# Where matmul inputs begin in SBUF: a pad in the first block, rows of 784 columns in the second, and one wider matmul at its end

## The chip, the cores and the metric

One core of a Trainium2 chip runs the whole kernel. The metric is the device time of one execution in microseconds (us). Three runs of the kernel before gave 3038.32, 3041.43 and 3042.83 us; the median is 3041.43 us.

## What is computed

Two transformer blocks stand one after the other, in float32. The first has two layers over 512 tokens of width 1024; each has a mixer (latent attention, pooling, gating) and a SwiGLU feed-forward of 2816 inner features:

```python
for l in range(DEPTH):
    h = rmsnorm(x, mix_norm[l])
    ...
    x = x + jnp.einsum('bsn,nd->bsd', mix, w_o[l])
    h = rmsnorm(x, ffn_norm[l])
    g = jnp.einsum('bsd,df->bsf', h, w_gate[l])
    u = jnp.einsum('bsd,df->bsf', h, w_up[l])
    x = x + jnp.einsum('bsf,fd->bsd', jax.nn.silu(g) * u, w_down[l])
```

The second has two layers over 256 context tokens and 512 latent tokens together, each input shifted and scaled by a condition vector; the last layer gives latent tokens alone:

```python
x = x + g2 * rmsnorm_2(swiglu(modulate(x, norm_g[l, 2], sh2, sc2), ffn_w_in[l], ffn_w_out[l]), norm_g[l, 3])
if need_ctx:
    ctx = ctx + cg2 * rmsnorm_2(swiglu(modulate(ctx, ...), ffn_w_in[l], ffn_w_out[l]), norm_g[l, 3])
```

## The kernel before, in words

Features lie on the 128 partitions, tokens along the row. Every float32 operand is held as a high and a low part (`h` and `l`, type float32r), and each product is three matmuls: high weight by high input, high by low, low by high (`mm`, L329 to L331, in the first block; `mm2`, L993, in the second; `sums`, L1542, and `first2`, L961, for parts of the tokens at a time). The stationary operand is a 128x128 block of weights, the moving operand 256, 258 or 512 tokens. Weights stream in through `wload`: a DMA into `raw`, ScalarE writes `whi`, VectorE `wlo`, two buffers of each. TensorE's order is written out by hand; the order on the other engines comes from a scheduler.

Where things begin in a row of SBUF (bytes within a partition, as the built program places them):

- **Weights.** The pool starts at 19968 = 39x512 and its tiles are 4096 bytes, so every block of 128 weights begins at a multiple of 512.
- **First block.** Mixer inputs `hah`/`hal` start at 48640 = 95x512, 2048 bytes each: multiples of 512. The feed-forward inputs `hbh`/`hbl` and inner features `hidh`/`hidl` stand in a pool that is stacked from the right under `blk1` (x, bt, acc: 20480 bytes under 229344), so all of them begin 480 bytes past a multiple of 512. The mixer's query tiles `qh`/`ql` begin 160 past one.
- **Second block.** `hh` and `hl` hold 8 rows (one for each 128 features) of 770 columns: 256 context tokens, 2 columns for the shift vectors, 512 latent tokens. A row is 3080 bytes = 6x512+8, so row k of `hh` begins 8k past a multiple of 512 and row k of `hl` 64+8k; latent tokens begin at column 258, 8 bytes further. `mm2` runs over `SEG`: 258 columns (context and shifts), then 512 (latent); over `SEGL`, in latent-only stages: 258 (shifts and 256 tokens), then 256.
- **Inner features of the second block** are arena tiles `t` of 780 columns; context and latent parts are written with the same two-column gap, so the parts begin at 64j and at 64j+8 past a multiple of 512.

In `ffn2` the down projection of the latent-only layer runs over `hseg` of two times 256 columns, into two PSUM banks (`mmtile`), although both halves have the same weights.

Of the kernel before, what the change touches and what calls it, by code (L numbers as in the profile page):

```python
# [9 lines left out]
F32 = mybir.dt.float32  # L10
# [7 lines left out]
P = 128  # L18
S = 512
SC = 256  # L20
T2 = S + SC
KD = 8
NF = 22
EPS = 1e-6
# [231 lines left out]
class Body:  # L256
# [171 lines left out]
    def mixer1(self, l, h, acc):  # L428
# [6 lines left out]
        W = S + 16  # L435
        X = lambda n=S, dt=F32: p.tile([P, W], dt, tag="t", bufs=XS, name=self.nm("t"))[:, :n]
        vcol = lambda n, j: self.vec1[:, vb + V1[n] + j:vb + V1[n] + j + 1]
        rc = T("rc", 1, (P, 8))

        def column(dst, src):  # L440

# [114 lines left out]
        def attend(h_, qp, po):  # L556


            j, hh = h_ // 2, h_ % 2
            (qh, ql), kt = qT[h_], kT[h_]  # L560
            prs = []
            for q in range(2):
                pss = self.aux()
                s = slice((2 * qp + q) * P, (2 * qp + q + 1) * P)
                self.mm(pss, qh[:, s], ql[:, s], kt[0], kt[1], True, True)
                sc = T("smx", 6, (P, 4))
                nc.vector.tensor_reduce(sc[:, 0:1], pss, AX.X, ALU.max, negate=True)
                pr = X()
                nc.scalar.activation(pr, pss, AF.Exp, bias=sc[:, 0:1], accum_out=sc[:, 1:2])
                nc.vector.reciprocal(sc[:, 2:3], sc[:, 1:2])  # L570
                if q == 0:
                    nc.scalar.activation(pr, pr, AF.Copy, scale=sc[:, 2:3])
                else:
                    nc.gpsimd.tensor_tensor(pr, pr, sc[:, 2:3].to_broadcast([P, S]), ALU.mult)
                prs.append(pr)
            yield
            yield
            pth, ptl = R("pth", 3, (P, 4, 256)), R("ptl", 3, (P, 4, 256))
            for q, pr in enumerate(prs):
                pt = self.aux()  # L580
                for k in range(4):
                    nc.tensor.transpose(pt[:, k * P:(k + 1) * P], pr[:, k * P:(k + 1) * P], self.ident)
                s = slice(q * P, (q + 1) * P)
                self.split(pth[:, :, s], ptl[:, :, s], pt.rearrange("p (k q) -> p k q", k=4))
            yield
            if qp == 0:
                po[h_] = self.aux()
            s = slice(qp * 256, qp * 256 + 256)
            for k in range(4):
                for e, pt in enumerate((pth, ptl)):  # L590
                    nc.tensor.matmul(po[h_][:, s], vv[:, k, h_ * P:(h_ + 1) * P], pt[:, k, :],
                                     start=(k == 0 and e == 0 and qp == 0), stop=(k == 3 and e == 1), skip_group_check=True)
            if qp == 1:
                t, pv = X(), po.pop(h_)
                o, o2 = slice(64 * hh, 64 * hh + 64), slice(64 - 64 * hh, 128 - 64 * hh)
                nc.scalar.activation(t[o], pv[o2], AF.Copy)
                nc.vector.tensor_tensor(t[o], pv[o], t[o], ALU.add)
                self.split(h[j][0][o], h[j][1][o], t[o], nc.gpsimd)
# [199 lines left out]
    def run(self):  # L798
# [4 lines left out]
        self.x = [xall[:, k, :] for k in range(KD)]  # L803
        self.bt = pb.tile([P, S], F32, tag="bt", name="bt")
        acc = pb.tile([P, S], F32, tag="acc", name="acc")
        ea = ExitStack()
        pa = ea.enter_context(tc.tile_pool(name="ha", bufs=1))
        ha = [(pa.tile([P, S], F32R, tag=f"hah{k}", name=f"hah{k}"), pa.tile([P, S], F32R, tag=f"hal{k}", name=f"hal{k}"))
# [83 lines left out]

    def shift2(self, l, m):
        sh = self.ada[l][:, m * 8:m * 8 + 8, :]
        self.split(self.hh[:, :, SC:SC + 2], self.hl[:, :, SC:SC + 2], sh)

    def squares2(self, k, x, o, w, acc, tmp=None):

# [12 lines left out]
    def feed2(self, k, x, o, w, l, n):  # L911

        for c, s in ((0, 1), (SC, 0)):
            a, b = max(o, c), min(o + w, (SC, T2)[1 - s])
            if a < b:
                h = a + (0, 2)[1 - s]
                self.split_scaled(self.hh[:, k, h:h + b - a], self.hl[:, k, h:h + b - a], x[:, a - o:b - o],
                                  self.mod[l][n][:, k, s:s + 1])

# [10 lines left out]
            nc.scalar.activation(acc[:, a:a + 256], ps[:, :256], AF.Ln, scale=1.0 / div, bias=self.epsc)  # L930
        nc.scalar.activation(acc[:, o:o + w], acc[:, o:o + w], AF.Exp, scale=-0.5)  # L931

    SEG = ((0, SC + 2), (SC + 2, S))
    SEGL = ((SC, SC + 2), (2 * SC + 2, SC))

    def proj2(self, seg, key, u=0):

# [4 lines left out]
        self.mm2(ps, wh, wl, 0, [(self.hh[:, k, :], self.hl[:, k, :]) for k in range(KD)], seg)  # L942
        return ps

    PART = ((0, 0, 0, SC + 2), (1, 0, SC + 2, SC), (1, SC, 2 * SC + 2, SC))
    PARTL = ((0, 0, SC, SC + 2), (1, 0, 2 * SC + 2, SC))

    def first2(self, parts, units, pend):

# [36 lines left out]
    def mm2(self, ps, wh, wl, off, xs, seg):  # L986
        t = self.nc.tensor
        n = len(xs)
        for k, (xh, xl) in enumerate(xs):
            s = slice(off + k * P, off + (k + 1) * P)  # L990
            for w, x, st, en in ((wh, xh, k == 0, False), (wh, xl, False, False), (wl, xh, False, k == n - 1)):
                for b, (o, w_) in enumerate(seg):
                    t.matmul(ps[:, b, :w_], w[:, s], x[:, o:o + w_], start=st, stop=en, skip_group_check=True)  # L993
            self.tick()
# [38 lines left out]
    def mixer_ab(self, r):  # L1033
# [420 lines left out]
        def place(h):  # L1454

            for a, n in ((0, 2), (2, 4)):
                hc = (slice(0, SC), slice(SC + 2, T2 + 2))[a // 2]
                self.split(self.hh[:, h, hc], self.hl[:, h, hc], gates[h][0][:, a * P:(a + n) * P])

        for h in range(3):  # L1460
# [16 lines left out]
        for h in range(8):  # L1477
# [1 line left out]
                for _ in finish(h):  # L1479
                    pass  # L1480
            place(h)
        return [(self.hh[:, h, :], self.hl[:, h, :]) for h in range(8)]

    SEGM = ((0, SC), (SC + 2, S))

    def post(self, ys, off, o, w, acc, mod, feed, sums=None):

# [41 lines left out]
    def sums(self, ws, xs, o, w):  # L1529

        t = self.nc.tensor
        ps = [self.aux() for _ in ws]
        n = len(xs)
        for ks in (range(n - 1), range(n - 1, n)):
            for p, (wh, wl, off) in zip(ps, ws):
                for k in ks:
                    xh, xl = xs[k]
                    s = slice(off + k * P, off + (k + 1) * P)
                    for i, (a, x) in enumerate(((wh, xh), (wh, xl), (wl, xh))):
                        for b in range(0, w, SC):  # L1540
                            c = o + b + (0, 2)[o + b >= SC]
                            t.matmul(p[:, b:b + SC], a[:, s], x[:, c:c + SC], start=(k == 0 and i == 0 and b == 0),  # L1542
                                     stop=(k == n - 1 and i == 2), skip_group_check=True)
                    self.tick()
        return [p[:, :w] for p in ps]
# [18 lines left out]
    def ffn2(self, l, r, seg, lat, parts, acc, post):  # L1564
# [3 lines left out]
        if lat:  # L1568
            cols = ((slice(SC, 2 * SC), 0, 2, 0), (slice(2 * SC, T2), 1, 0, 0))
            bcol = slice(0, 2)  # L1570
            hseg = ((SC + 2, SC), (2 * SC + 2, SC))
        else:
            cols = ((slice(0, SC), 0, 0, 1), (slice(SC, T2), 1, 0, 0))
            bcol = slice(SC, SC + 2)
            hseg = self.SEGM
        hid = []

        def unit(f):
# [13 lines left out]
            for c, b, p0, s in cols:  # L1592
                n = c.stop - c.start
                nc.vector.tensor_tensor(u[:, c], pu[:, b, p0:p0 + n], r[:, c], ALU.mult)
                nc.vector.scalar_tensor_tensor(a[:, c], u[:, c], bu[:, s:s + 1], a[:, c], ALU.add, ALU.mult)  # L1595
                h0 = hseg[b][0]
                self.split(hi[:, h0:h0 + n], lo[:, h0:h0 + n], a[:, c])
            hid.append((hi, lo))

        f = 0  # L1600
        for gi, g in enumerate(GROUPS):
# [6 lines left out]
            for d in range(0, KD, 2):  # L1608
                wh, wl = self.wload("w2", ("d", l, gi), d // 2, 2 * g * P)
                for i in range(2):  # L1610
                    ps = self.mmtile()
                    self.mm2(ps, wh, wl, i * g * P, hid[:g], hseg)
                    k = d + i
                    if gi == 0:
                        ys[k] = self.T()
                    for c, b, p0, s in cols:
                        n = c.stop - c.start
                        if gi == 0:
                            nc.scalar.activation(ys[k][:, c], ps[:, b, :n], AF.Copy)
                        else:  # L1620
                            nc.vector.tensor_tensor(ys[k][:, c], ys[k][:, c], ps[:, b, :n], ALU.add)
# [22 lines left out]
    def mixer_c(self, r):  # L1644
# [96 lines left out]
        held = []  # L1741

        def store(h, o):
            hc = slice(SC + 2, T2 + 2)
            self.split(self.hh[:, h, hc], self.hl[:, h, hc], o)

        def attend(h, qp):
# [54 lines left out]
        for n in range(2 * 16 + 4):  # L1802
# [7 lines left out]
                store(*held.pop(0))  # L1810
            if n == 1 or n % 4 == 0 and 0 < n <= 20:
                late.pop(0)()
        return [(self.hh[:, h, :], self.hl[:, h, :]) for h in range(8)]

    def arena(self, name, slots, width=780):
        es = ExitStack()
        self.ar = es.enter_context(self.tc.tile_pool(name=name, bufs=1, reuse_waits="tile"))
        self.nslots = slots
# [3 lines left out]
    def second_begin(self):  # L1822
# [2 lines left out]
        self.e2 = ExitStack()  # L1825
        pb = self.e2.enter_context(tc.tile_pool(name="blk2", bufs=1, reuse_waits="tile"))
        self.dr = self.e2.enter_context(tc.tile_pool(name="dram", bufs=1, space=bass.MemoryType.DRAM))
        self.hh = pb.tile([P, KD, T2 + 2], F32R, tag="hh", name="hh")
        self.hl = pb.tile([P, KD, T2 + 2], F32R, tag="hl", name="hl")
        self.accs = [pb.tile([P, T2], F32, tag=f"acc{i}", name=f"acc2{i}") for i in range(2)]  # L1830
        es = ExitStack()
        p = es.enter_context(tc.tile_pool(name="ctx0", bufs=1, reuse_waits="tile"))
# [9 lines left out]
    def second(self, xall, pf, hb, acc, ef, eb):  # L1842
# [57 lines left out]
        self.drain()  # L1900
        ea.close()

        ea = self.arena("ffn20", 25)
        self.ffn2(0, n0, self.SEG, False, ((0, SC), (SC, SC), (S, SC)), na,
                  lambda ys, o, w: self.post(ys, 0, o, w, na, self.mod[0][3], feed(1, 0), n0))
        self.first2(self.PART, (("ck", 0), ("ck", 1)), norms)
# [17 lines left out]
        self.drain()  # L1924
        ea.close()

        ea = self.arena("ffn21", 26)

        def store(k, x, o, w):
            if k % 2:  # L1930
# [36 lines left out]
```

## Time and profile before

| | us |
|---|---|
| median of three runs | 3041.43 |
| profiled execution, its own time | 3047.24 |
| its span in the trace | 3045.4 |
| TensorE (PE) busy in the span | 2920.7 |
| VectorE (DVE) busy | 1862.0 |
| ScalarE (ACT) busy | 1191.7 |

The profiled execution is 5.8 us above the median, and 1.8 us of it lie outside the span. Matmuls overlap in the trace: the next one starts before the shown end of the one ahead, so how fast they follow each other is read from starts, over a stretch with a known number of them.

### The profile page before, as it was taken

What the parts mean: (1) busy time and instruction counts of PE and PEld (TensorE: products, weight loads), DVE (VectorE), ACT (ScalarE), POOL (GpSimd) and SP (SyncE); (2) the same over time, 40 slices, a digit from 0 to 9 for tenths busy, and PEclk for the clock granted to TensorE, in tenths of its full rate; (3) what the DMA queues carried; (4) which work ended last, traced back from release to release, by engine and by line L of the source; (5) the groups of instructions that cost most, each with busy time, mean ns of one, the idle gap of its engine ahead of it and who ended that gap; (6) DMA issues with size and microseconds to landing.
All of it is one profiled execution on the core that took longest, in us unless ns stands there. A gap on an engine that the chain in (4) does not pass through costs nothing. (4 is left out here: it accounts for less than half of the span.)

```text
span 3045.4 us, 42771 instructions
## 1 busy us (share of the span) xinstructions
PE 2920.7 (96%) x17002; PEld 2499.6 (82%) x17002; DVE 1862.0 (61%) x3253; ACT 1191.7 (39%) x2088; POOL 550.1 (18%) x434
## 2 busy tenths in 40 slices
PE   9989999999999999899999989999999899999997
PEld 7777888777778888766767888888889788899997
DVE  7679974476689965746554653333344778544445
ACT  5663222346642223432325543221123577532222
POOL 3630000046310001432233140000001420300002
PEclk9999999999999999899999999999999999999999
DMA  4236653232156632210121302212221210223322
GB/s 150 63 103 191 208 159 97 87 107 63 56 190 209 206 124 97 72 42 28 35 66 60 106 20 70 63 63 63 63 63 63 81 43 13 91 94 93 95 91 70
DMA packets 85112, 278.49 MB, mean 91 GB/s; under 512 B 9968, under 2 KB 15344, under 8 KB 84400
## 3 DMA queue, kind: packets, MB, share of 16 engines
q1 hardware_dynamic: 84912, 275.76, 28.6%
q8 instruction: 134, 2.20, 0.3%
q14 instruction: 66, 0.54, 0.1%
HBM read 264.84 MB, written 6.68 MB: 89 GB/s over the span
## 5 line engine op out<-in xcount | busy, mean ns | idle before, releaser
L302 ACT ACTIVATE whi<-raw 128x1024 fp32r<-128x1024 f32 (+1 forms) x363 | 377.7, 1041 | 1289.7 <-PE b L993 472.3
L993 PE MATMUL b<-hh,whi 128*128 128x258 f32 x2000 | 491.1, 327 | 0.0
L993 PE MATMUL b<-hl,whi 128*128 128x258 f32 x2000 | 470.9, 317 | 0.0
L993 PE MATMUL b<-hh,wlo 128*128 128x258 f32 x2000 | 469.7, 316 | 0.0
L303 DVE TENSOR_TENSOR wlo<-raw,whi 128x1024 fp32r<-128x1024 f32 (+1 forms) x321 | 398.0, 1240 | 108.9 <-ACT whi L302 107.5
L993 PEld LDWEIGHTS b<-hh,whi 128*128 128x128 f32 x2000 | 339.8, 190 | 45.3 <-issue 23.8
L993 PEld LDWEIGHTS b<-hl,whi 128*128 128x128 f32 x2000 | 351.3, 190 | 26.1
L993 PEld LDWEIGHTS b<-hh,wlo 128*128 128x128 f32 x2000 | 350.7, 189 | 26.7
L330 PE MATMUL b<-hbl,whi 128*128 128x512 f32 x704 | 279.3, 397 | 3.5 <-DVE hbl L341 3.5
L329 PE MATMUL b<-hbh,whi 128*128 128x512 f32 x704 | 279.8, 398 | 0.8 <-ACT hbh L340 0.8
L331 PE MATMUL b<-hbh,wlo 128*128 128x512 f32 x704 | 279.3, 397 | 0.7 <-DVE wlo L303 0.7
L859 DVE SCALAR_TENSOR_TENSOR junk<-araw,cond 128x1024 f32<-128x1024 f32 x192 | 238.6, 1243 | 4.7 <-DMA araw<-ada 1.9
L1527 POOL TENSOR_TENSOR acc<-acc,t 128x256 f32<-128x256 f32 (+1 forms) x54 | 48.9, 906 | 1018.3 <-ACT t L1522 1017.4
L993 PE MATMUL b<-t,whi 128*128 128x256 f32 (+1 forms) x1152 | 217.3, 311 | 0.0
L993 PEld LDWEIGHTS b<-t,whi 128*128 128x128 f32 x1152 | 178.1, 190 | 12.6
L388 POOL TENSOR_TENSOR acc<-acc,sq 128x512 f32<-128x512 f32 (+1 forms) x33 | 44.4, 1346 | 786.3 <-ACT sq L385 785.8
L330 PEld LDWEIGHTS b<-hbl,whi 128*128 128x128 f32 x704 | 132.5, 188 | 36.7 <-DVE hbl L341 4.2
L329 PEld LDWEIGHTS b<-hbh,whi 128*128 128x128 f32 x704 | 132.7, 188 | 33.6 <-ACT hbh L340 1.2
L331 PEld LDWEIGHTS b<-hbh,wlo 128*128 128x128 f32 x704 | 132.6, 188 | 33.5 <-DVE wlo L303 1.6
L303 POOL TENSOR_TENSOR wlo<-raw,whi 128x1024 fp32r<-128x1024 f32 x42 | 105.3, 2510 | 249.1 <-ACT whi L302 194.7
L331 PE MATMUL b<-hidh,wlo 128*128 128x512 f32 (+1 forms) x352 | 136.0, 386 | 1.6 <-DVE wlo L303 1.6
L329 PE MATMUL b<-hidh,whi 128*128 128x512 f32 (+1 forms) x352 | 135.7, 386 | 0.0
(444 smaller groups left out, 5805.1 us busy)
## 6 DMA issues: line engine op xcount, KB each, us to landing
raw<-w SPq DMA_DIRECT2D x365, 512.0 KB, 3.6
araw<-ada SPq DMA_DIRECT2D x96, 512.0 KB, 4.1
raw<-w SPq DMA_DIRECT2D x18, 256.0 KB, 2.7
xr<-xd SPq DMA_DIRECT2D x2, 2048.0 KB, 8.3
t<-dm SPq DMA_DIRECT2D x8, 384.0 KB, 5.3
x<-xT SPq DMA_DIRECT2D x8, 256.0 KB, 5.2
kTh<-krh SPq DMA_DIRECT2D x32, 64.0 KB, 2.0
kTl<-krl SPq DMA_DIRECT2D x32, 64.0 KB, 2.0
```

The costliest lines, as they stand in the source:

```text
L302: self.last = nc.scalar.activation(hi[:, :m], r, AF.Copy).ins
L303: self.lo_eng.tensor_tensor(lo[:, :m], r, hi[:, :m].bitcast(F32), ALU.subtract)
L329: t.matmul(out, ah, bh, start=start, stop=False, skip_group_check=True)
L330: t.matmul(out, ah, bl, start=False, stop=False, skip_group_check=True)
L331: t.matmul(out, al, bh, start=False, stop=stop, skip_group_check=True)
L388: nc.gpsimd.tensor_tensor(acc[:, c], acc[:, c], t[:, c], ALU.add)
L859: nc.vector.scalar_tensor_tensor(junk, raw, 1.0, self.cond[:, s], ALU.mult, ALU.mult, accum_out=self.ada[l][:, t, s:s + 1])
L993: t.matmul(ps[:, b, :w_], w[:, s], x[:, o:o + w_], start=st, stop=en, skip_group_check=True)
L1527: nc.gpsimd.tensor_tensor(ac, ac, t, ALU.add)
```

## The change

It moves starting addresses, and makes one pair of matmuls a single one. No computed value changes.

1. `run`: a tile of 120 floats (480 bytes) that nothing uses is put below `acc`, so the pool under it begins at 126464 = 247x512. `hbh`, `hbl`, `hidh`, `hidl` now begin at multiples of 512. In `mixer1` two small tiles (`rc`, `smx`) get wider; the query tiles go from 160 to 192 past one.
2. `hh` and `hl` have rows of 784 columns = 3136 bytes = 6x512+64. Context begins at column 14 (`CO`), shifts stand at 270 (`SH`), latent tokens at 272 (`LT`). In row k of either, the 258-column part begins 64k+56 past a multiple of 512, the latent part 64k+64.
3. In the two feed-forwards of the second block the arena tiles are 768 columns without a gap: both parts begin at multiples of 512. Elsewhere the arena's 780 becomes 784.
4. In the latent-only layer `hseg` is one segment of 512 columns and one bank; the evacuation that follows is one instruction over 512 columns.

```diff
+CO, SH, LT, HW = 14, 270, 272, 784
...
+        pb.tile([P, 120], F32, tag="pad", name="pad")
...
-    SEG = ((0, SC + 2), (SC + 2, S))
-    SEGL = ((SC, SC + 2), (2 * SC + 2, SC))
+    SEG = ((CO, SC + 2), (LT, S))
+    SEGL = ((SH, SC + 2), (LT + SC, SC))
...
-    SEGM = ((0, SC), (SC + 2, S))
+    SEGM = ((0, SC), (SC, S))
...
         if lat:
             cols = ((slice(SC, 2 * SC), 0, 2, 0), (slice(2 * SC, T2), 1, 0, 0))
             bcol = slice(0, 2)
-            hseg = ((SC + 2, SC), (2 * SC + 2, SC))
+            hseg, outs = ((SC, S),), ((slice(SC, T2), 0),)
         else:
...
-            hseg = self.SEGM
+            hseg, outs = self.SEGM, ((slice(0, SC), 0), (slice(SC, T2), 1))
...
-                h0 = hseg[b][0]
-                self.split(hi[:, h0:h0 + n], lo[:, h0:h0 + n], a[:, c])
-            hid.append((hi, lo))
+                self.split(hi[:, c], lo[:, c], a[:, c])
+            hid.append((hi, lo, 0, 0))
...
-                    ps = self.mmtile()
+                    ps = self.mmtile() if len(hseg) > 1 else Banks(self.aux())
...
-                    for c, b, p0, s in cols:
+                    for c, b in outs:
...
-    def arena(self, name, slots, width=780):
+    def arena(self, name, slots, width=784):
...
-        self.hh = pb.tile([P, KD, T2 + 2], F32R, tag="hh", name="hh")
-        self.hl = pb.tile([P, KD, T2 + 2], F32R, tag="hl", name="hl")
+        self.hh = pb.tile([P, KD, HW], F32R, tag="hh", name="hh")
+        self.hl = pb.tile([P, KD, HW], F32R, tag="hl", name="hl")
...
-        ea = self.arena("ffn20", 25)
+        ea = self.arena("ffn20", 25, T2)
...
-        ea = self.arena("ffn21", 26)
+        ea = self.arena("ffn21", 26, T2)
```

The order of instructions differs in one place alone, the down projections of the last feed-forward (`ffn2` with `lat`). On TensorE there, before, first output of the second group of inner features (`b` is a PSUM bank, `t` an inner feature's high or low tile):

```order
L993 MATMUL b_23791<-t_23087,whi_23786 128x256
L993 MATMUL b_23792<-t_23087,whi_23786 128x256
L993 MATMUL b_23791<-t_23088,whi_23786 128x256
L993 MATMUL b_23792<-t_23088,whi_23786 128x256
L993 MATMUL b_23791<-t_23087,wlo_23787 128x256
L993 MATMUL b_23792<-t_23087,wlo_23787 128x256
```

The same place on TensorE with the change:

```order
L997 MATMUL b_23728<-t_23088,whi_23723 128x512
L997 MATMUL b_23728<-t_23089,whi_23723 128x512
L997 MATMUL b_23728<-t_23088,wlo_23724 128x512
L997 MATMUL b_23728<-t_23316,whi_23723 128x512
L997 MATMUL b_23728<-t_23317,whi_23723 128x512
```

Each pair of 256 columns into two banks has become one matmul of 512 columns into one bank. On VectorE behind them, before (`t` is now the output being summed):

```order
L1621 TENSOR_TENSOR t_23117<-t_23117,b_23791 128x256
L1621 TENSOR_TENSOR t_23117<-t_23117,b_23792 128x256
L1621 TENSOR_TENSOR t_23134<-t_23134,b_23819 128x256
L1621 TENSOR_TENSOR t_23134<-t_23134,b_23820 128x256
L303 TENSOR_TENSOR wlo_23911<-raw_23909,whi_23910 128x1024
```

And on VectorE with the change:

```order
L1624 TENSOR_TENSOR t_23111<-t_23111,b_23728 128x512
L1624 TENSOR_TENSOR t_23120<-t_23120,b_23742 128x512
L305 TENSOR_TENSOR wlo_23792<-raw_23790,whi_23791 128x1024
L1624 TENSOR_TENSOR t_23135<-t_23135,b_23762 128x512
L1624 TENSOR_TENSOR t_23144<-t_23144,b_23776 128x512
```

Two additions of 256 columns have become one of 512; the weight preparation (`wlo`) stands between the same outputs as before. In all there are 432 matmuls and 32 VectorE additions fewer.

## Rows read from the trace of the kernel before

**Rows 1.** The page's first part: busy time, share of the span, instructions.

```profile
PE 2920.7 (96%) x17002; PEld 2499.6 (82%) x17002; DVE 1862.0 (61%) x3253; ACT 1191.7 (39%) x2088; POOL 550.1 (18%) x434
```

**Rows 2.** Stretches: length; busy PE, PEld, DVE, ACT, POOL; PE clock, DMA share, GB/s.

```profile
245.00:600.00 355.00, 351.21 (x1495) 281.85 (x1496) 251.17 (x357) 95.81 (x113) 1.06 (x1) 1.00 0.47 149
810.00:1215.00 405.00, 403.56 (x1823) 328.46 (x1823) 311.50 (x450) 130.46 (x175) 26.68 (x25) 1.00 0.51 162
1262.00:1720.00 458.00, 438.09 (x2494) 322.23 (x2495) 251.29 (x591) 182.97 (x341) 140.53 (x76) 0.97 0.15 45
1825.00:2360.00 535.00, 534.88 (x3118) 472.26 (x3117) 213.25 (x378) 133.15 (x200) 10.23 (x13) 1.00 0.21 64
2660.00:3005.00 345.00, 345.00 (x2875) 345.00 (x2874) 162.64 (x340) 106.44 (x168) 0.00 (x0) 1.00 0.30 92
```

**Rows 3.** PE's largest wait from 830 to 1190 us: total, times, longest.

```profile
PE b L331 <- DVE wlo L303: 0.9, 2, 0.5
```

**Rows 4.** Stretches of TensorE in the first block that hold 512-column matmuls alone.

```profile
58.84:63.05 4.21, 4.21 (x19) 1.00 0.58 154
63.05:84.59 21.54, 21.54 (x97) 1.00 0.37 115
292.42:605.55 313.13, 313.13 (x1344) 1.00 0.45 143
888.71:1190.17 301.46, 301.46 (x1293) 1.00 0.54 171
```

**Rows 5.** Timeline of TensorE where the first two of these stretches meet.

```profile
62.82 0.39 PE L331 MATMUL b<-qh,wlo 128*128 128x512 f32 x1
63.05 0.39 PE L329 MATMUL b<-hah,whi 128*128 128x512 f32 x1
```

**Rows 6.** Matmul groups by form: tiles, shapes, count, busy us, mean ns.

```profile
L329 PE MATMUL b<-hbh,whi 128*128 128x512 f32 x704 | 279.8, 398 | 0.8 <-ACT hbh L340 0.8
L329 PE MATMUL b<-hidh,whi 128*128 128x512 f32 x320 | 126.6, 395 | 0.0
L993 PE MATMUL b<-hh,whi 128*128 128x258 f32 x1000 | 302.9, 303 | 0.0
L993 PE MATMUL b<-hh,whi 128*128 128x512 f32 x600 | 237.9, 397 | 0.0
L993 PE MATMUL b<-hh,whi 128*128 128x256 f32 x400 | 112.7, 282 | 0.0
L993 PE MATMUL b<-t,whi 128*128 128x256 f32 x864 | 173.9, 283 | 0.0
L993 PE MATMUL b<-t,whi 128*128 128x512 f32 x288 | 107.4, 394 | 0.0
```

**Rows 7.** Stretches of TensorE in the second block's feed-forwards, each of pairs alone.

```profile
1879.39:1946.84 67.45, 67.45 (x385) 1.00 0.21 67
1946.84:1980.60 33.76, 33.76 (x194) 1.00 0.19 63
2691.59:2737.62 46.03, 46.03 (x386) 1.00 0.32 104
2737.62:2760.81 23.19, 23.19 (x194) 1.00 0.30 91
```

**Rows 8.** Feature row 7's pairs, 258+512: sum of 32 stretches, 1886.77 to 2250.41.

```profile
sum 33.28, PE 33.28; mean PE 1.04
```

**Rows 9.** The same for feature row 0, 32 stretches, 1879.39 to 2243.05.

```profile
sum 34.09, PE 34.09; mean PE 1.07
```

**Rows 10.** Feature row 7's pairs, 258+256: sum of 32 stretches, 2696.64 to 2945.12.

```profile
sum 22.86, PE 22.86; mean PE 0.71
```

**Rows 11.** The same for feature row 2, 32 stretches, 2693.03 to 2941.53.

```profile
sum 23.51, PE 23.51; mean PE 0.73
```

**Rows 12.** VectorE's additions to the outputs, 2660 to 3005, and 1860 to 2355 us.

```profile
L1621 DVE TENSOR_TENSOR t<-t,b 128x256 f32<-128x256 f32 x64 | 24.1, 418 | 40.8 <-PE b L993 40.8
L1621 DVE TENSOR_TENSOR t<-t,b 128x512 f32<-128x512 f32 x32 | 21.8, 680 | 0.0
```

More of the change, by code (lines that the diff above doesn't have):

```diff
@@ L437, in mixer1 @@
         vcol = lambda n, j: self.vec1[:, vb + V1[n] + j:vb + V1[n] + j + 1]
-        rc = T("rc", 1, (P, 8))
+        rc = T("rc", 1, (P, 16))
         def column(dst, src):
@@ L565, in attend @@
                 self.mm(pss, qh[:, s], ql[:, s], kt[0], kt[1], True, True)
-                sc = T("smx", 6, (P, 4))
+                sc = T("smx", 6, (P, 16))
                 nc.vector.tensor_reduce(sc[:, 0:1], pss, AX.X, ALU.max, negate=True)
@@ L894, in shift2 @@
         sh = self.ada[l][:, m * 8:m * 8 + 8, :]
-        self.split(self.hh[:, :, SC:SC + 2], self.hl[:, :, SC:SC + 2], sh)
+        self.split(self.hh[:, :, SH:LT], self.hl[:, :, SH:LT], sh)
     def squares2(self, k, x, o, w, acc, tmp=None):
@@ L915, in feed2 @@
             if a < b:
-                h = a + (0, 2)[1 - s]
+                h = a + (LT - SC, CO)[s]
                 self.split_scaled(self.hh[:, k, h:h + b - a], self.hl[:, k, h:h + b - a], x[:, a - o:b - o],
@@ L943, in proj2 @@
         return ps
-    PART = ((0, 0, 0, SC + 2), (1, 0, SC + 2, SC), (1, SC, 2 * SC + 2, SC))
-    PARTL = ((0, 0, SC, SC + 2), (1, 0, 2 * SC + 2, SC))
+    PART = ((0, 0, CO, SC + 2), (1, 0, LT, SC), (1, SC, LT + SC, SC))
+    PARTL = ((0, 0, SH, SC + 2), (1, 0, LT + SC, SC))
     def first2(self, parts, units, pend):
@@ L988, in mm2 @@
         n = len(xs)
-        for k, (xh, xl) in enumerate(xs):
+        for k, (xh, xl, *_) in enumerate(xs):
             s = slice(off + k * P, off + (k + 1) * P)
@@ L1456, in place @@
             for a, n in ((0, 2), (2, 4)):
-                hc = (slice(0, SC), slice(SC + 2, T2 + 2))[a // 2]
+                hc = (slice(CO, SH), slice(LT, HW))[a // 2]
                 self.split(self.hh[:, h, hc], self.hl[:, h, hc], gates[h][0][:, a * P:(a + n) * P])
@@ L1481, in mixer_ab @@
             place(h)
-        return [(self.hh[:, h, :], self.hl[:, h, :]) for h in range(8)]
-    SEGM = ((0, SC), (SC + 2, S))
+        return [(self.hh[:, h, :], self.hl[:, h, :], CO, LT - SC) for h in range(8)]
+    SEGM = ((0, SC), (SC, S))
     def post(self, ys, off, o, w, acc, mod, feed, sums=None):
@@ L1536, in sums @@
                 for k in ks:
-                    xh, xl = xs[k]
+                    xh, xl, *at = xs[k]
                     s = slice(off + k * P, off + (k + 1) * P)
@@ L1540, in sums @@
                         for b in range(0, w, SC):
-                            c = o + b + (0, 2)[o + b >= SC]
+                            c = o + b + at[o + b >= SC]
                             t.matmul(p[:, b:b + SC], a[:, s], x[:, c:c + SC], start=(k == 0 and i == 0 and b == 0),
@@ L1743, in store @@
         def store(h, o):
-            hc = slice(SC + 2, T2 + 2)
+            hc = slice(LT, HW)
             self.split(self.hh[:, h, hc], self.hl[:, h, hc], o)
@@ L1812, in mixer_c @@
                 late.pop(0)()
-        return [(self.hh[:, h, :], self.hl[:, h, :]) for h in range(8)]
-    def arena(self, name, slots, width=780):
+        return [(self.hh[:, h, :], self.hl[:, h, :], CO, LT - SC) for h in range(8)]
+    def arena(self, name, slots, width=784):
         es = ExitStack()
```

## The prediction

> **What bounds the kernel.** I began with busy time: TensorE is busy for 96% of the span [rows 1]. Split by stage, the four feed-forward stretches are the plainest: TensorE is busy for 351.2 of 355, 403.6 of 405, 534.9 of 535 and 345 of 345 us at full clock, while VectorE, the next, has 251.2, 311.5, 213.3 and 162.6 [rows 2]. In the second of them TensorE's largest kind of wait sums to 0.9 us [rows 3]. There the end is set by how fast one matmul follows another; whatever is shortened between starts comes off the time.
>
> So I read the pace, from stretches that hold one kind of matmul and no wait. The number in brackets counts instructions seen in a stretch, one or two more than the intervals. 18 matmuls of 512 columns with inputs `qh`/`ql`, 160 bytes past a multiple of 512, take 4.21 us: 233.9 ns each. The next 96, inputs `hah`/`hal` at multiples of 512, take 21.54 us for 95 intervals: 226.7 ns [rows 4]. They follow each other directly [rows 5]: same weights' buffers, same shape, same clock, other starts. In the feed-forward, inputs at 480 past, 1342 intervals take 313.13 us and 1292 take 301.46: 233.3 ns both times [rows 4]. The weights begin at multiples of 512 in all of them. The reader is to see two paces, 227 and 233 to 234, that go with the starting address.
>
> In the second block the eight feature rows begin at eight offsets, and the pace goes with the row. A pair of 258 and 512 columns takes 67.45 us / 192 = 351.3 ns on the mean [rows 7]; in row 7, whose parts begin at 56 and 64 (`hh`) or 120 and 128 (`hl`), 33.28 / 96 = 346.7 [rows 8]; in row 0, at 0 and 8 or 64 and 72, 34.09 / 96 = 355.1 [rows 9]. Pairs of 258 and 256 take 46.03 / 192 = 239.7 on the mean [rows 7], 22.86 / 96 = 238.1 in row 7 [rows 10], 23.51 / 96 = 244.9 in row 2 [rows 11].
>
> **The change part by part.**
>
> *The pad.* `hb` and `hid` go from 480 to 0 past a multiple of 512, which is where `ha` is. There are 3 x 704 and 3 x 320 = 3072 such matmuls of 512 columns, the named groups standing for a third each [rows 6]. 3072 x (233.3 - 226.7) = 20.3 us. Bounds: nothing, if it is the tiles and not the offset, and this; I take 19.5, since the 226.7 is the best of the `ha` stretches and others may lie some tenths above. VectorE would be busy for 311.5 of some 397 us instead of 405, so nothing else becomes the bound.
>
> *Rows of 784 columns.* Every row now has the 258 part at 56 and the latent part at 0 past a multiple of 64, as only row 7 had before. 3 x 600 = 1800 pairs of 258 and 512 [rows 6] at row 7's pace would give 1800 x 4.6 = 8.3 us; 3 x 400 = 1200 pairs of 258 and 256 would give 1200 x 1.6 = 1.9 us. But row 7 shows only offsets 64 and 128 past a multiple of 512; the new rows also stand at 192 to 448, which no row of before shows for 512 columns. The bounds are row 7's pace for all, and the worst row's: 1800 x (351.3 - 355.1) = -6.8 and 1200 x (239.7 - 244.9) = -6.2 us. Nearest to row 7, but not all of it: 2.8 ns and 1.0 ns a pair, 5.0 and 1.2 us. Of the 1800, 744 are in the mixer (31 projections of 24), where TensorE is busy for 438.1 of 458 us [rows 2] and waits between; I take 1.0 us off for that.
>
> *Inner features without a gap.* In the context layer 432 pairs (288 with `whi` [rows 6], half as many with `wlo`) of 256 and 512 columns take 33.76 / 96 = 351.7 ns [rows 7]. Now both parts begin at multiples of 512: the 512 at 226.7, the 256 at half of a pair of 256 columns, 23.19 / 96 / 2 = 120.8 [rows 7], together 347.5. Gain 4.2 x 432 = 1.8 us, between 0 and that; I take 1.4.
>
> *One matmul for two.* 864 and 432 matmuls of 256 columns, less the 288 and 144 of the context layer [rows 6], are 864 in 432 pairs of 241.6 ns; each becomes one matmul of 512 at 226.7. Gain 14.9 x 432 = 6.4 us; at 233.3 it would be 3.6. I take 6.2.
>
> *Costed at nothing.* 64 VectorE additions of 418 ns become 32 of 680 [rows 12]: 26.8 us against 21.8, under a VectorE that is idle for half of that stretch. A bank is then read 0.68 us after its last matmul instead of 0.42; with eight banks and one filled in 12 x 227 ns = 2.7 us, TensorE doesn't come to wait for it. The pad and the wider small tiles issue nothing. No other instruction moves on any engine.
>
> Sum: 19.5 + 5.0 + 1.2 - 1.0 + 1.4 + 6.2 = 32.3 us. The profiled execution's 3047.2 (span 3045.4 and 1.8 outside it) becomes 3014.9; it lies 5.8 us above the median, so the median 3041.4 becomes 3009.1.
>
> **A rule against it.** Where the 18 and the 96 matmuls meet, the pace changes from 233.9 to 226.7 ns with the address [rows 4, 5]. The Trainium skill (TensorE: Matmul & The Clock Gate, "Step-by-step: what each phase is for") says that TensorE has two independent read ports, so that loading the next weights takes no read bandwidth from the running matmul; by that, where inputs and weights begin relative to each other would not matter. The row disagrees, and decides here; by the rule alone the sum would be the merged matmuls' 3.6 to 6.4 us, the second rival below.
>
> **Rivals.**
>
> *The new rows are bad ones.* For it: paces differ by 8 ns between rows for no reason that the profile names [rows 8, 9], and 192 to 448 are untried. Against: the one class that resembles them is the fastest. If they cost what the worst rows do, 5.0 + 1.2 - 1.0 turns into -13.0: the gain is 14.1 us, 3027.3. Chance 0.10.
>
> *Addresses set nothing; only the matmul count does.* Then `ha` would be faster for what it is, not for where. Against: `qh` beside it [rows 4], and eight paces in eight rows of one tile. Gain 6.2 us, 3035.2. Chance 0.05.
>
> *Equal starts collide, and it gets slower.* Inputs and weights begin alike modulo 512 after the change; far more matmuls would read the same offset at once. Against: `ha` is in that position already, at 226.7. For the whole to be slower by 6.1 us, with the rows' and gaps' terms as above (6.6), 512-column matmuls at offset 0 must cost more than X with 3072 x (X - 233.3) + 432 x (X - 241.6) = 12.7 us, X = 237.9 ns. At 240, 20.6 - 0.7 - 6.6 = 13.3 us more: 3054.7. Chance 0.03.
>
> The forecast has 0.82, and by itself 3002 to 3016: its upper side is rows that give nothing (3014.3) with two us of scatter between runs, its lower side row 7's pace everywhere (3041.4 - 20.3 - 8.3 - 1.9 - 1.8 - 6.4 = 3002.7). The range for 8 in 10 goes from 3001 up to 3019, to hold part of the first rival; what lies above it is the rest of that one and the other two, and some misses below. A measurement of this kernel can tell 0.2%, 6.1 us. Faster by more: the forecast, the first rival and about half of the second, whose 6.2 us stand on the edge: 0.94. Within: 0.03. Slower: 0.03.
>
> **What would show it.** In the feed-forwards of the first block, 512-column matmuls that follow each other every 227 ns; each of those two stretches about 9 to 10 us shorter. In the context layer, 24 pairs of one projection in about 8.36 us instead of 8.43. In the last layer, 96 matmuls of 512 columns in 21.8 us where 96 pairs took 23.2. The order of instructions and the waits stay as they are. The forecast is wrong if `hb` stays at 233 with its new address, or if single rows of `hh` take 355 ns a pair or more; the profile after shows the pace of each row apart.

## The result and the profile after

The kernel after takes 3013.79 us (median of four runs, 3008.93 to 3015.0); the kernel before, run beside it, 3041.23 (3038.32 to 3042.83). The ratio is 0.9906, 95% interval 0.9894 to 0.9918: faster by 0.9%. The profiled execution took 3015.0 us with a span of 3012.8, where that of before had 3045.4: 32.6 us less. The medians differ by only 27.4, because the profiled execution of before lay 6.0 us above the median of these four runs and that of after 1.2 above its own.

The page's first part, busy time of each engine in the kernel after:

```profile
PE 2885.2 (96%) x16570; PEld 2465.0 (82%) x16570; DVE 1861.2 (62%) x3221; ACT 1191.3 (40%) x2080; POOL 548.8 (18%) x434
```

Against [rows 1] TensorE has 432 matmuls fewer and is busy for 35.5 us less; its share is 96% as before. Weight loads (PEld) shrink with it, and VectorE, ScalarE and GpSimd moved by no more than 1.3 us.

Stretches of TensorE alone in the kernel after: length, busy time with the number of instructions seen, granted clock, DMA share, GB/s. The first three answer to [rows 4], the others to [rows 7], in the same order.

```profile
62.23:83.78 21.55, 21.55 (x96) 1.00 0.36 113
288.65:592.86 304.21, 304.21 (x1344) 1.00 0.47 147
875.63:1168.51 292.88, 292.88 (x1294) 1.00 0.54 176
1858.92:1926.22 67.30, 67.30 (x385) 1.00 0.22 68
1926.22:1959.51 33.29, 33.29 (x194) 1.00 0.21 64
2665.56:2711.32 45.76, 45.76 (x386) 1.00 0.33 104
2711.32:2733.10 21.78, 21.78 (x98) 1.00 0.32 96
```

Divide by the intervals, as before. The 95 of `ha` are unchanged at 226.8 ns. In the first block's feed-forwards 304.21 us / 1342 and 292.88 / 1292 give 226.7 ns twice, where 233.3 stood: the two paces have become one. In the second block 67.30 / 192 = 350.5 ns a pair of 258 and 512 columns (351.3 before), 33.29 / 96 = 346.8 a pair of inner features (351.7), 45.76 / 192 = 238.3 a pair of 258 and 256 (239.7), and 21.78 / 96 = 226.9 for one matmul of 512 where 241.6 was paid for two of 256. The 351.7 of before is one of five stretches, and they differ; here are the other four:

```profile
1862.54:1879.39 16.85, 16.85 (x98) 1.00 0.38 108
2048.05:2081.65 33.60, 33.60 (x193) 1.00 0.20 63
2149.12:2182.95 33.83, 33.83 (x194) 1.00 0.20 63
2250.41:2283.92 33.51, 33.51 (x193) 1.00 0.20 63
```

With 48 pairs in the first and 96 in each of the others, they run from 349.1 to 352.4 ns; the mean of all 432 pairs is 350.8.

TensorE's largest wait from 815 to 1168 us in the kernel after (total, times, longest), and the timeline where `qh`/`ql` and `ha` meet:

```profile
PE b L333 <- DVE wlo L305: 2.2, 4, 0.7
```

```profile
61.99 0.39 PE L333 MATMUL b<-qh,wlo 128*128 128x512 f32 x1
62.23 0.39 PE L331 MATMUL b<-hah,whi 128*128 128x512 f32 x1
62.45 0.40 PE L332 MATMUL b<-hal,whi 128*128 128x512 f32 x1
```

The largest kind of wait was 0.9 us in all in [rows 3]: a faster TensorE now waits 1.3 us more for `wlo`, in a stretch of 353 us. Nothing new bounds it. The step from one pace to the other is still there, as in [rows 5].

Matmuls of the inner features as `mm2` issues them, from 1820 us on, and VectorE's additions to the outputs, both in the kernel after:

```profile
L997 PE MATMUL b<-t,whi 128*128 128x512 f32 x576 | 195.1, 390 | 0.0
```

```profile
L1624 DVE TENSOR_TENSOR t<-t,b 128x512 f32<-128x512 f32 x32 | 21.9, 686 | 38.0 <-PE b L997 38.0
```

With `whi` there are 288 + 288 of 512 columns ([rows 6] had 288, and 576 halves more), and the additions of the last layer are 32 of 686 ns, as [rows 12] led one to expect.

### The profile page after: what moved, and what is told of

Same layout as the page of the kernel before. It is cut to its first block, busy times and chain, and to the rows that moved or that the text cites. A ratio compares the mean times of both kernels' runs of the same rounds, so it can differ in the third digit from the quotient of the medians.

```text
span 3012.8 us, 41854 instructions
## 1 busy us (share of the span) xinstructions
PE 2885.2 (96%) x16570; PEld 2465.0 (82%) x16570; DVE 1861.2 (62%) x3221; ACT 1191.3 (40%) x2080; POOL 548.8 (18%) x434
## 5 line engine op out<-in xcount | busy, mean ns | idle before, releaser
L305 DVE TENSOR_TENSOR wlo<-raw,whi 128x1024 fp32r<-128x1024 f32 (+1 forms) x321 | 398.2, 1241 | 103.7 <-ACT whi L304 103.1
L332 PE MATMUL b<-hbl,whi 128*128 128x512 f32 x704 | 275.1, 391 | 3.6 <-DVE hbl L343 3.6
L331 PE MATMUL b<-hbh,whi 128*128 128x512 f32 x704 | 275.6, 391 | 1.0 <-ACT hbh L342 1.0
L333 PE MATMUL b<-hbh,wlo 128*128 128x512 f32 x704 | 274.9, 391 | 0.9 <-DVE wlo L305 0.9
L863 DVE SCALAR_TENSOR_TENSOR junk<-araw,cond 128x1024 f32<-128x1024 f32 x192 | 238.3, 1241 | 7.3 <-DMA araw<-ada 3.7
L997 PEld LDWEIGHTS b<-t,whi 128*128 128x128 f32 x864 | 151.8, 188 | 22.8
L332 PEld LDWEIGHTS b<-hbl,whi 128*128 128x128 f32 x704 | 132.7, 188 | 32.4 <-DVE hbl L343 4.4
L333 PEld LDWEIGHTS b<-hbh,wlo 128*128 128x128 f32 x704 | 132.7, 189 | 29.4 <-DVE wlo L305 1.8
L331 PEld LDWEIGHTS b<-hbh,whi 128*128 128x128 f32 x704 | 132.7, 188 | 29.1 <-ACT hbh L342 1.4
L333 PE MATMUL b<-hidh,wlo 128*128 128x512 f32 (+1 forms) x352 | 134.2, 381 | 2.9 <-DVE wlo L305 2.9
L331 PE MATMUL b<-hidh,whi 128*128 128x512 f32 (+1 forms) x352 | 133.8, 380 | 0.0
```

The source lines that it names most:

```text
L305: self.lo_eng.tensor_tensor(lo[:, :m], r, hi[:, :m].bitcast(F32), ALU.subtract)
L331: t.matmul(out, ah, bh, start=start, stop=False, skip_group_check=True)
L332: t.matmul(out, ah, bl, start=False, stop=False, skip_group_check=True)
L333: t.matmul(out, al, bh, start=False, stop=stop, skip_group_check=True)
L863: nc.vector.scalar_tensor_tensor(junk, raw, 1.0, self.cond[:, s], ALU.mult, ALU.mult, accum_out=self.ada[l][:, t, s:s + 1])
```

## Experiments

What was open: whether the address sets the pace at all, or the tile; whether it is the input's place, or its distance from the weights' place; which modulus counts; and why the rows of 784 columns gave so little. "Place" is the start of the input's row less the start of the weights, in bytes. Paces by place are mean differences between a matmul's start and the next one's in the trace, over intervals without a wait. Dots in an edit stand for lines left out.

**Without the pad**, the rest of the change as it is.

```diff
-        pb.tile([P, 120], F32, tag="pad", name="pad")
```

> The change without its 120-float pad, so hb and hid begin 480 bytes past a multiple of 512 again; all else as in the change. If the address sets their pace: 512-column matmuls of the first block's feed-forwards start every 233.3 ns again and the time rises by 3072 x 6.6 ns = 20.3 us, to about 3034. If it was something else in the change (the wider small tiles, other placements), they stay at 226.7 ns and 3014 us.

Measured 3031.06 us (3028.65 to 3036.43), 0.997 of before (0.9961 to 0.998). The stretches of the first block in this kernel:

```profile
62.42:84.21 21.79, 21.79 (x98) 1.00 0.40 116
291.29:604.66 313.37, 313.37 (x1344) 1.00 0.45 143
887.46:1189.15 301.69, 301.69 (x1294) 1.00 0.53 171
```

One interval more in each than above: 313.37 / 1343 and 301.69 / 1293 = 233.3 ns again, `ha` stays at 227. The pad alone is worth 17.3 us by the medians, the rest of the change 9.9. The paces make it 20.3. Part of the gap is TensorE's clock, which stood at the lower of its two levels, 1.2 GHz, for 107 us in this profile and for 114 in that of the change. The tile theory is out: same tiles, same instructions, another start.

**The weights moved by 64 bytes**, and with them `ha`, `hh` and `hl`; `hb` and `hid` stay where the change put them.

```diff
+        self.pc.tile([P, 16], F32, tag="wpad", name="wpad")
```

> A tile of 16 floats ahead of the weights moves weights, ha, hh and hl by 64 bytes; hb and hid stay at multiples of 512. Theory A, only the distance of inputs and weights modulo 512 counts: ha (64 against 64) keeps 226.7 ns, hb and hid (0 against 64) slow to 231 to 234 ns, about +17 us. Theory B, only where the inputs themselves begin counts: hb and hid keep 226.7 ns, ha (now at 64) slows to 231 ns or so, +4 us. Theory C, both must begin at multiples of 512: both slow, +20 us.

One run of 3031.12 us. The same stretches in this kernel:

```profile
62.83:84.64 21.81, 21.81 (x98) 1.00 0.36 116
291.76:605.11 313.35, 313.35 (x1344) 1.00 0.45 143
888.25:1189.94 301.69, 301.69 (x1294) 1.00 0.53 171
```

`hb` and `hid`, whose own addresses did not change, are back at 233.3 ns, and `ha`, which moved along with the weights, keeps 227.2. It is the distance between the two that counts, theory A. The Trainium skill (TensorE: Matmul & The Clock Gate, "Step-by-step: what each phase is for") gives inputs and weights a read port each, so that loading takes nothing from the running matmul; moving the weights alone would then have cost nothing. The measurement differs by 6.6 ns a matmul, and decides.

**Every row of `hb` at another place**: a tile of 64 bytes behind each pair, so row k stands at 64k.

```diff
...
+                pf.tile([P, 16], F32, tag=f"hpad{k}", name=f"hpad{k}")
...
```

> Feature row k of hb begins 64k bytes past a multiple of 512 (16-float tiles between the rows); hid and weights stay at multiples of 512. Theory M512, the place modulo 512 counts: row 0 at 226.7 ns, the others between 229 and 235 ns each with its own pace, 2112 x 7/8 x 5 ns = +9 us. Theory M64, a start at a multiple of 64 is enough: all rows at 226.7 ns, no change of the time.

One run of 3020.18 us. Mean pace in ns of the three matmuls of a row (L331 with `hbh`, L332 with `hbl`, L333 with `hbh`):

| place | 0 | 64 | 128 | 192 | 256 | 320 | 384 | 448 |
|---|---|---|---|---|---|---|---|---|
| L331 | 226.2 | 232.3 | 232.5 | 229.6 | 226.1 | 231.7 | 232.6 | 228.5 |
| L332 | 234.5 | 233.6 | 233.8 | 233.5 | 235.7 | 233.4 | 232.5 | 233.3 |
| L333 | 228.2 | 233.0 | 231.8 | 233.4 | 228.4 | 233.4 | 231.6 | 233.4 |

Rows k and k+4 read alike: the pattern repeats after 256 bytes, which neither theory had. Only at 0 and 256 are two of the three fast, so a multiple of 64 is not enough. That L332 is slow at 0 too, where the change has it at 227, was not foreseen. Here the rows ahead are slow ones; whether that is the reason is not shown.

**`hb` and `hid` at 256, and at 128**: the pad is 56 or 88 floats.

```diff
-        pb.tile([P, 120], F32, tag="pad", name="pad")
+        pb.tile([P, 56], F32, tag="pad", name="pad")
```

> The pad has 56 floats: hb and hid begin 256 bytes past a multiple of 512, weights at multiples of 512. Period 256: 226.7 ns as in the change, 3014 us. Period 512: 231 to 235 ns, up to +20 us.

> The pad has 88 floats: hb and hid begin 128 bytes past a multiple of 512 all through the run. If the period were 128, 226.7 ns and 3014 us; if it is 256, 231 to 235 ns, +13 to +25 us.

One run each: 3007.24 us at 256, 3027.29 at 128. The second feed-forward at 256, then at 128:

```profile
873.11:1166.24 293.13, 293.13 (x1295) 1.00 0.55 176
```

```profile
879.67:1180.13 300.46, 300.46 (x1294) 1.00 0.53 171
```

Over 1293 intervals that is 226.7 and 232.4 ns. 256 is as good as 0; 128 is hardly better than the 233.3 of 480.

**`hbl` alone at 128, in layer 0 only.**

```diff
...
+                if l == 0:
+                    pf.tile([P, 32], F32, tag=f"hpad{k}", name=f"hpad{k}")
+                hb.append((hi, pf.tile([P, S], F32R, tag=f"hbl{k}", name=f"hbl{k}")))
...
```

> In the first layer alone the low tiles hbl begin 128 bytes past a multiple of 512, the high tiles hbh stay at multiples of it; the second layer is as in the change. Theory D, each matmul's pace is its own place's: hbh keeps 226.7 ns, hbl takes the steady pace of 128 (e7). Theory R, a matmul that stands elsewhere costs its neighbours too: hbh of the first layer slows as well, all three of a product between 229 and 236 ns, in the second layer none does; about +5 us.

One run of 3011.72 us. Timeline of layer 0 in this kernel:

```profile
300.66 0.39 PE L331 MATMUL b<-hbh,whi 128*128 128x512 f32 x1
300.89 0.40 PE L332 MATMUL b<-hbl,whi 128*128 128x512 f32 x1
301.12 0.39 PE L333 MATMUL b<-hbh,wlo 128*128 128x512 f32 x1
301.35 0.39 PE L331 MATMUL b<-hbh,whi 128*128 128x512 f32 x1
301.57 0.40 PE L332 MATMUL b<-hbl,whi 128*128 128x512 f32 x1
301.81 0.39 PE L333 MATMUL b<-hbh,wlo 128*128 128x512 f32 x1
```

The three repeat every 0.69 us, where three at 226.7 ns take 0.68. In the means from 286 to 600 us `hbl` takes 234.1 ns and the two `hbh` 226.8 and 225.8: the matmul that was moved pays, and its neighbours at 0 don't, theory D, though it pays 1.7 ns more than at 128 throughout. Taken with the L332 of the spread rows: among the places tried for `hb`, 0 or 256 is needed for the steady 226.7 ns, but not always enough.

**Rows of 800 and of 832 columns**, to bring more parts to good places: with 800 the rows stand 128 apart, with 832 the parts are at 0 modulo 256, all but the 258-column part of the latent-only stages, which stands at 248 (columns from 318). The context part begins at column 0 and the shifts are written behind it as well.

```diff
-CO, SH, LT, HW = 14, 270, 272, 784
+CO, SH, LT, HW = 0, 318, 320, 832   # or 0, 286, 288, 800
...
```

> Rows of 800 columns: context at column 0, shifts at 256 (and, where the latent-only part needs them, again at 286), latent tokens at 288. All starts of context and latent parts are multiples of 128 past 512; the 258-column part of the latent-only stages starts at 120 past a multiple of 128. Theory S, the 258-column part's start at 56 past a multiple of 64 is what keeps pairs at 350.5 ns: pairs of 258 and 512 fall to 347 to 348 ns, 1800 x 3 ns = -5 us, 258 and 256 stay at 238. Theory L, the 258 columns or the alternation of two tokens' ranges keep them there: 350.5 ns on the mean and no change of the time (0 +- 2 us).

> Rows of 832 columns = 13 x 256 bytes: context at column 0 (shifts behind it at 256 and, for the latent-only stages, again at 318), latent tokens at 320. Both parts of every row stand at the weights' place modulo 256. (The ada step's unused product is written as bfloat16 to make room; its sum, which counts, stays float32.) Theory P, a run of matmuls is fast when all of them stand at the weights' place modulo 256 and any other place in the run costs it: pairs of 258 and 512 fall from 350.5 to 347 to 348 ns in all rows, pairs of 258 and 256 from 238.4 to 236.3 in all rows, 1800 x 3 + 1200 x 2 = -8 us against the change, about 3006. Theory L, the 258 columns or the alternation of two ranges set it: 350 to 351 and 238 on the mean, 3014.

800: 3017.39 us (3016.13 to 3020.91), 0.9927 (0.991 to 0.9943). 832: 3014.21 (3007.39 to 3017.39), 0.9912 (0.9896 to 0.9929). Neither beats the change beyond its scatter. Pairs of 258+512 and of 258+256 with rows of 800:

```profile
1861.25:1928.66 67.41, 67.41 (x385) 1.00 0.21 68
2671.74:2717.61 45.87, 45.87 (x386) 1.00 0.34 104
```

They take 351.1 and 238.9 ns, near the change's 350.5 and 238.3, so it is not the start at 56 (theory S) that keeps pairs of 258+512 from row 7's pace. Pairs of 258+512, of inner features, and of 258+256, with rows of 832:

```profile
1849.32:1917.16 67.84, 67.84 (x385) 1.00 0.22 68
1917.16:1950.44 33.28, 33.28 (x193) 1.00 0.19 64
2658.77:2704.44 45.67, 45.67 (x386) 1.00 0.34 105
```

353.3, 346.7 and 237.9 ns. With both parts at place 0 the 258+512 pairs are slower than in the change (350.5), which neither theory had, though 256+512 at the same places take 6.6 ns less. What place 0 does for 512 columns that follow each other, it does not do here.

**The first part 256 columns long** in the context stages, in those rows of 832. This kernel leaves out what the two shift columns give to the results.

```diff
-    SEG = ((CO, SC + 2), (LT, S))
+    SEG = ((CO, SC), (LT, S))
...
```

> The rows of 832 columns with every 512-column part at place 0 (pairs 353.1 and 237.9 ns, 3014 us), but with the first part 256 columns long in place of 258. It leaves out what the two shift columns give to the results: a fixed pair of columns is added in their place. Theory that the length of the part ahead decides: the pairs now take what 256+512 took in the inner features, 346.7 ns, so 1800 x 6.4 = 11.5 us less, and some 3000 us or below. Theory that it doesn't: two columns fewer are 0.9 ns at 2.4 GHz, so 352.2 and 237.0 ns a pair, 2.7 us in all, and about 3011 us.

One run of 2998.75 us. The same three stretches:

```profile
1847.22:1913.78 66.56, 66.56 (x386) 1.00 0.22 70
1913.78:1947.06 33.28, 33.28 (x194) 1.00 0.22 64
2650.57:2696.23 45.66, 45.66 (x385) 1.00 0.34 104
```

66.56 / 192 = 346.7 ns: here the length decides. Two columns, 0.9 ns if 512 take 226.7, cost 6.6 ns a pair. The span is 8.9 us shorter than with 258 columns (2996.6 to 3005.5), less than 1800 x 6.6 = 11.9: in the mixer, where other matmuls stand between, pairs without a wait go from 352.5 to 349.5 ns only. The 258+256 pairs, whose length stayed, stayed at 237.8.

**Rows of 832 columns with every row at the place that was cheapest before**, 72 and 80. The ada step's product is bfloat16 here too, which leaves its VectorE time as it was (1241 and 1242 ns).

```diff
-CO, SH, LT, HW = 14, 270, 272, 784
+CO, SH, LT, HW = 18, 274, 276, 832
...
```

> Rows of 832 columns, with the 258-column part of every row at place 72 and the 512-column part at place 80 modulo 256 bytes, which was the cheapest place of the sixteen in the trace of before (347.0 ns a pair 258+512, 232.6 ns a pair 258+256, as against means of 351.3 and 239.7). Theory that a pair's time belongs to its place alone: every pair takes 347.0 and 232.6 ns; against the change (350.5 and 238.3 ns) that is 1800 x 3.5 + 1200 x 5.7 = 13 us, so about 3000 us. Rival, that a pair's time also hangs on what ran just before it, which is now always a row at the same place where before it was a row 8 bytes earlier: pairs near 350 to 353 and 238 ns, and about 3014 us, the change's own time.

Measured 3006.86 us (3004.54 to 3010.26), 0.989 of before (0.9873 to 0.9907): the fastest of the kernels that leave nothing out and have several runs, 6.9 us under the change's median, though the intervals of the two ratios overlap. Its stretches: inner features, 258+512, inner features, 258+512, 258+256:

```profile
1836.56:1853.20 16.64, 16.64 (x97) 1.00 0.33 103
1853.20:1919.77 66.57, 66.57 (x386) 1.00 0.22 70
1919.77:1953.68 33.91, 33.91 (x193) 1.00 0.21 63
1953.68:2020.88 67.20, 67.20 (x385) 1.00 0.21 63
2660.15:2704.95 44.80, 44.80 (x385) 1.00 0.35 107
```

The 258+256 pairs take 233.3 ns, near the 232.6 that the place gave before. The first stretch of 258+512 takes 346.7, as the place theory says, but the next one, with the same rows at the same places, 350.0; and the inner features, which this edit does not touch, go from 346.7 to 353.2 between 1836 and 1920 us and stay there in all four later stretches. So place and length alone do not set the pace. That it hangs on what ran ahead, as the rival had it, fits but is not shown. Worked out against the change: 1800 x (350.8 - 348.9, the means over all) + 1200 x (238.3 - 233.3) - 384 x (353.2 - 346.8) = 3.4 + 6.0 - 2.5 = 6.9 us. The profiled spans differ by 10.0 (3012.8 and 3002.8); TensorE is idle for 3.4 us less of this one (124.2 against 127.6).

**Two matmuls for one again** in the last layer, the rest as in the change.

```diff
-            hseg, outs = ((SC, S),), ((slice(SC, T2), 0),)
+            hseg, outs = ((SC, SC), (2 * SC, SC)), ((slice(SC, 2 * SC), 0), (slice(2 * SC, T2), 1))
```

> The change with one part undone: the inner features of the last block go as two matmuls of 256 columns again, no gap between them, in place of one of 512. By the prediction's price a pair takes 240 to 241.6 ns and the one matmul 226.9, so 432 x 13.1 to 14.7 = 5.7 to 6.4 us slower than the change: 3019.5 to 3020.2 us, 0.993 of before. Rival, that the two weight loads in place of one are hidden beside the matmuls: no more than 432 x 2 = 0.9 us slower, 3014.7 us.

Measured 3017.68 us (3007.97 to 3018.93), 0.9915 (0.9895 to 0.9935): 3.9 us slower than the change by the medians, less than the scatter of four runs can tell. The paces settle it; 258+256, then the 96 pairs of 256:

```profile
2664.57:2710.36 45.79, 45.79 (x386) 1.00 0.32 104
2710.36:2733.40 23.04, 23.04 (x194) 1.00 0.30 92
```

23.04 / 96 = 240.0 ns for a pair against 226.9 for the one: 432 x 13.1 = 5.7 us. The second matmul is not free. Whether its weight load, its issue or the change of bank costs the 13.1 ns is not separated here.

## Why the prediction was right, and where a size was off

3013.79 us lies in the range of 3001 to 3019 and in the forecast's own of 3002 to 3016; the likeliest time, 3009.1, was 4.7 us low. By its terms, each with the paces of the profiles:

| term | predicted, us | measured, us |
|---|---|---|
| the pad | 19.5 | 3072 x (233.3 - 226.7) = 20.3 |
| rows of 784, pairs of 258+512, mixer taken off | 5.0 - 1.0 | 1800 x (351.3 - 350.5) = 1.4 |
| rows of 784, pairs of 258+256 | 1.2 | 1200 x (239.7 - 238.3) = 1.7 |
| inner features without a gap | 1.4 | 432 x (350.8 - 346.7) = 1.8 |
| one matmul for two | 6.2 | 432 x (241.4 - 226.9) = 6.3 |
| sum | 32.3 | 31.5 |

The last two terms use the mean of all their stretches. That the sums lie 0.8 us apart is in part luck: the pairs of 258 and 512 gave 2.6 us less than was taken, and the other four terms 0.8, 0.5, 0.4 and 0.1 more.

- **What bounds it** held: the paces explain 31.5 of the 32.6 us between the spans. TensorE is idle for 2.9 us more (span less busy time, 124.7 to 127.6), and was at the lower clock for 5 us less.
- **The pad** held to the last digit of a pace, and undoing it alone brings 233.3 ns back. The prediction counted modulo 512; 256 is what the runs show, and the place of the weights is the other half of the rule.
- **Rows of 784** were mis-sized: 0.8 ns a pair of 258+512 in place of 2.8. The step that failed is "nearest to row 7, but not all of it". By place of the 512 part the pairs take 348.6 (64), 350.5 (128), 350.6 (192), 353.5 (256), 348.8 (320), 350.4 (384), 350.8 (448) and 353.2 ns (0). Again it repeats after 256 bytes. Row 7's own places, 64 and 128, are the better ones, and their repeats 320 and 384, untried before, are as good; 192 and 448 are near them, and 256 and 0, the best for 512 columns alone, the worst. But at row 7's own places the pairs now take 348.6 and 350.5 ns, where row 7 took 346.7 [rows 8]. So its pace did not come with its place, and the step was wrong in that also, not only for the untried places. The first rival was partly there: the two rows' terms gave 3.1 us in place of 5.2, about a tenth of the way to its -13.0.
- **The gap and the one matmul for two** came in at or just above what was taken. The gap's 351.7 was read from one stretch of five. It was not undone by itself and rests on the paces.
- **Its signs.** The two stretches of the first block are 8.9 and 8.6 us shorter (9 to 10 were named), the 96 matmuls take 21.78 us as named, and 24 pairs of a projection 67.30 / 8 = 8.41 us, not 8.36. ScalarE also has 8 instructions fewer, which was not costed.
- **The second rival** (addresses set nothing) fell to the experiment without the pad, **the third** (equal starts collide) to 226.7 ns at equal starts.
- **The 4.7 us** between 3009.1 and the median are not in the paces: the profiled execution was to become 3014.9 and took 3015.0. The step that failed is the last one, which carried the distance of one profiled execution from its median (5.8 us) over to the changed kernel, whose own profile lies 1.2 above; in the rows of 832 it lies 6.8 below. The time at the lower clock differs from one execution to the next: 119 us of the span in the profile of before, 114 in that of after, 97 to 129 in the experiments'. In that of after one long piece of it stands in the last mixer, here as stretches of TensorE ahead of it, in it and behind it (the fourth column is the granted clock):

```profile
1632.00:1639.00 7.00, 6.07 (x35) 1.00 0.26 77
1639.00:1653.00 14.00, 14.00 (x47) 0.51 0.00 0
1653.00:1660.00 7.00, 7.00 (x40) 1.00 0.00 0
```

At 0.51, the 1.2 GHz level, 47 instructions pass in 14 us where 40 pass in 7 behind it: some 6 us are lost, by this estimate. Ahead of it stands a wait of 0.93 us for `mC`, but the same wait of 0.9 to 1.0 us is in all thirteen profiles, so it does not settle it alone. The piece is in three of the twelve profiles of changed kernels (the change, `hb` at 128, rows at 72 and 80), at the same place of the program, and before has 3.4 us there. What decides is open. Single runs, as most of those above, are therefore read by their paces and not by their times.

## What to carry to other kernels

Where TensorE is the bound and matmuls follow each other without waits, read the pace from starts, by tile and by shape; where one shape has two paces, look at where its operands begin. Here it paid to put inputs of 512 columns at the weights' start modulo 256 bytes and to merge neighbouring halves that share weights. Look at lengths too: 258 columns for 256 cost as much as a bad place. A place that is good in one sequence is no promise in another, so measure each sequence of lengths by itself.

## What was not expected of the hardware

Paces stand on a lattice: 226.7, 233.3, 240.0, 346.7 and 353.3 ns are 34, 35, 36, 52 and 53 times 6.67 ns, which at the 2.4 GHz of these stretches is 16 cycles. Paces between the steps are means over a longer pattern, and the pattern takes whole steps: two pairs in the rows at 72 and 80 (350.0 = 52.5 steps), three pairs of 258+256 in the rows of 832 (713.3 ns, 107 steps), seven matmuls of `hb` and `hid` at 128 (1626.7 ns, 244 steps), and in the change's feed-forward twelve pairs of 258+512, which are four feature rows (4206.7 ns, 631 steps). That fits the two columns that cost a whole step, and a pace that is kept from one stretch to the next. No run shows the mechanism behind it, and what made the inner features change from 52 to 53 steps at 1920 us stays open.
